# Rotary embedding on one core: all DMAs through one ring, and the tables as 16 descriptors of 4 KB

## The chip, the cores and the metric

One core of a Trainium2 chip runs the kernel. The metric is the device time of one execution in microseconds (us). Besides that there is one profiled execution, whose span (first to last instruction) and own time are given below.

## What is computed

The input `x` is 16 x 512 x 1024 float32 (batch, position, 16 heads of 64). Each head's 64 values are two halves of 32, which are rotated by tables `cos` and `sin` of 512 positions x 32:

```python
x = x.reshape(batch, seq, num_heads, head_dim)
x1, x2 = x[..., :half_dim], x[..., half_dim:]
cos = cos[None, :, None, :]
sin = sin[None, :, None, :]
rotated = np.concatenate([
    x1 * cos - x2 * sin,
    x1 * sin + x2 * cos
], axis=-1)
```

Input and output are 33.55 MB each; each table is 64 KB.

## The kernel before

**Slabs.** The work is cut into eight slabs of 4 MB, numbered 0 to 7. A slab is 128 partitions x 8192 float32: 8 rows of 1024 in each partition. Three places on chip (`places`, L52) hold a pair of neighbouring slabs each: 0 and 1, 2 and 3, 4 and 5. Slabs 6 and 7 use the first place again, so loads 6 and 7 have to wait until stores 0 and 1 have left it. In DRAM a partition's 16 rows of a pair lie together (`there`, L59), so a DMA of one slab has 32 KB in each partition, and a DMA of a pair 64 KB.

**A slab's way.** ScalarE casts the slab from float32 to bf16 in place (`cast`, L132, by `copy`, L137). VectorE makes two multiplications with the tables (L152) and one addition of swapped halves (L155). ScalarE casts the result back to float32, into the same place (L158), and the slab is stored. Slab 0 is worked on in two parts of 4 rows, slab 7 in parts of 4, 2 and 2. ScalarE's casts are in an order written out by hand: the cast of the next slab stands ahead of the back-cast of the present one, so each of its rounds is cast(s+1), back-cast(s); for slab 7 all casts come ahead of the back-cast of slab 6.

**Tables.** `cos` and `sin` are loaded with 64 partitions x 1 KB each (L77 to L79), which is 8 positions in a partition. GpSimd builds selection matrices (`pick`, L87 to L95) and casts each table to bf16 (L99). TensorE spreads them to 128 partitions: for each parity of slab four matmuls with `pick` as weights (L106), into the column layout cos, cos, sin, -sin; -1 in `pick` makes the sign. VectorE copies the even slabs' table to bf16 (L113), ScalarE the odd slabs' (L144). No multiplication can start before the first copy.

**Queues and their order.** SyncE (SP) and ScalarE (ACT) each feed a ring of their own, and 16 DMA engines take packets from both. On SP: load 0, load 1, loads 2 and 3 in two DMAs of every second partition (L83), loads 4 and 5 in one DMA, all issued without a wait, then load 6 behind store 0, and load 7 behind store 1. On ACT: the tables (L78) at the start, then the stores of slabs 0 to 3 (L69), each behind its slab's back-cast in ScalarE's own sequence, the pair 4 and 5 in two halves (L162) and the pair 6 and 7 in one DMA.

The part of the changed function that sets the queues is short:

```python
def load(s, n=1):
    nc.sync.dma_start(out=here(s, n), in_=there(x, s, n))

def store(s, n=1):
    nc.scalar.dma_start(out=there(out_flat, s, n), in_=here(s, n))
```

Of the kernel before, what the change touches and what calls it, by code (L numbers as in the profile page):

```python
# [2 lines left out]

# [4 lines left out]


@with_exitstack  # L10
def kernel(
    ctx: ExitStack,
    tc: tile.TileContext,
    x: bass.AP,
    cos: bass.AP,
    sin: bass.AP,
    num_heads: int,
    out: bass.AP,
):
    nc = tc.nc  # L20
    P = nc.NUM_PARTITIONS

    batch, seq, dim = x.shape
    nh = num_heads
    hd = dim // nh
    half = hd // 2
    bf16 = mybir.dt.bfloat16
    f32 = mybir.dt.float32

    nb = 2  # L30
    nslabs = batch // nb
    rpp = nb * seq // P
    W = rpp * dim
    TP = seq // rpp
    TW = rpp * half

    out_flat = out.rearrange("b s h d -> b s (h d)")

    singles = ctx.enter_context(tc.tile_pool(name="singles", bufs=1))
    pairs = ctx.enter_context(tc.tile_pool(name="pairs", bufs=3))  # L40
    psum = ctx.enter_context(tc.tile_pool(
        name="psum", bufs=1, space=bass.MemoryType.PSUM))


    def view(t, offset, *dims):
        return dataclasses.replace(t, offset=t.offset + offset,
                                   ap=[t.ap[0], *[list(d) for d in dims]])

    places = [pairs.tile([P, 2 * W], f32, tag="pair", name="pair") for _ in range(3)]  # L52


    def here(s, n=1):
        return view(places[s // 2 % 3], s % 2 * W, (1, n * W))


    def there(t, s, n=1):  # L59
        return bass.AP(tensor=t.tensor, offset=t.offset + s // 2 * 2 * P * W + s % 2 * W,  # L60
                       ap=[[2 * W, P], [1, n * W]])


    def load(s, n=1):
        nc.sync.dma_start(out=here(s, n), in_=there(x, s, n))  # L65


    def store(s, n=1):
        nc.scalar.dma_start(out=there(out_flat, s, n), in_=here(s, n))  # L69


    load(0)


    cos_sb = singles.tile([TP, TW], f32, tag="cos_sb")
    sin_sb = singles.tile([TP, TW], f32, tag="sin_sb")
    for t, src in ((cos_sb, cos), (sin_sb, sin)):  # L77
        nc.scalar.dma_start(out=t, in_=bass.AP(  # L78
            tensor=src.tensor, offset=src.offset, ap=[[TW, TP], [1, TW]]))  # L79

    load(1)
    for p in range(2):
        nc.sync.dma_start(out=here(2, 2)[p::2], in_=there(x, 2, 2)[p::2])  # L83
    load(4, 2)


    pick = singles.tile([TP, 4 * P], bf16, tag="pick")  # L87
    nc.gpsimd.memset(pick, 0.0)  # L88
    for h in range(2):
        for g in range(2):  # L90
            part = view(pick, (2 * h + g) * P, (TP // 2, 2 * P // TP), (1, TP // 2))
            nc.gpsimd.affine_select(  # L92
                out=part, in_=part, compare_op=mybir.AluOpType.not_equal,
                fill=1.0 - 2.0 * g, base=-h, pattern=[[0, 2 * P // TP], [-2, TP // 2]],
                channel_multiplier=1)  # L95

    tab1 = singles.tile([TP, 2 * TW], bf16, tag="tab1")
    for i, t in enumerate((cos_sb, sin_sb)):
        nc.gpsimd.tensor_copy(out=view(tab1, i * TW, (1, TW)), in_=t)  # L99

    accs, tabs = [], []
    for h in range(2):
        acc = psum.tile([P, 2 * rpp * hd], f32, tag=f"acc{h}", name="acc")
        for i in range(2):
            for f in range(2):
                nc.tensor.matmul(  # L106
                    view(acc, i * rpp * hd + f * half, (hd, rpp), (1, half)),
                    view(pick, (2 * h + i * f) * P, (1, P)),
                    view(tab1, i * TW, (half, rpp), (1, half)),
                    start=True, stop=True)  # L110
        accs.append(acc)
        tabs.append(singles.tile([P, 2 * rpp * hd], bf16, tag=f"tab{h}", name="tab"))
    nc.vector.tensor_copy(out=tabs[0], in_=accs[0])  # L113

    passes = []
    for s in range(nslabs):
        r = 0  # L120
        for n in {0: (4, 4), nslabs - 1: (4, 2, 2)}.get(s, (rpp,)):
            passes.append((s, r, n))
            r += n


    def halves(u):
        s, r, n = u
        t = here(s).bitcast(bf16)
        return [view(t, (2 * r + i * n) * dim, (1, n * dim)) for i in range(2)]


    def cast(u):  # L132
        s, r, n = u
        copy(halves(u)[0], view(here(s), r * dim, (1, n * dim)))


    def copy(out, in_):  # L137
        tc.keep_in_program_order(nc.scalar.copy(out=out, in_=in_))  # L138


    ahead = list(passes)
    for _ in range(2):
        cast(ahead.pop(0))
    copy(tabs[1], accs[1])  # L144
    cast(ahead.pop(0))
    for i, u in enumerate(passes):
        s, r, n = u
        while ahead and len(passes) - len(ahead) < (i + 2 if s < nslabs - 2 else len(passes)):
            cast(ahead.pop(0))
        lo, up = halves(u)  # L150
        for t, a in ((up, 0), (lo, rpp * hd)):
            nc.vector.tensor_mul(  # L152
                out=t, in0=lo,
                in1=view(tabs[s % 2], a + r * hd, (hd, n), (0, nh), (1, hd)))
        nc.vector.tensor_add(  # L155
            out=up, in0=up, in1=view(lo, half, (hd, n * nh), (-half, 2), (1, half)))

        copy(view(here(s), r * dim, (1, n * dim)), up)  # L158
        if r + n == rpp:
            if s == 5:  # L160
                for p in range(2):
                    nc.scalar.dma_start(out=there(out_flat, 4, 2)[p::2], in_=here(4, 2)[p::2])  # L162
            elif s == 7:
                store(6, 2)
            elif s < 4:
                store(s)
            if s < 2:
                load(s + 6)


# [1 line left out]
_INS = ['x', 'cos', 'sin', 'num_heads']  # L172
_OUTS = [((16, 512, 16, 64), 'float32')]

_NUMBERS = {'num_heads': 16}


# [26 lines left out]
```

## Time and profile before

| what | value |
|---|---|
| median of 3 runs | 161.87 us (161.72 to 161.93) |
| profiled execution, its own time | 161.8 us |
| its span | 160.0 us |
| VectorE busy | 107.9 us (67%) |
| ScalarE busy | 114.3 us (71%) |
| packets of SP's queue (q1), share of 16 engines | 49.5% |
| packets of ACT's queue (q10), share of 16 engines | 48.7% |
| bytes moved | 67.24 MB, mean 420 GB/s |
| one cast of a slab on ScalarE | 7.02 us |
| one multiplication or addition of a slab on VectorE | 4.42 us |

The page's part 3 gives, for each DMA queue, the time of its packets as a share of 16 engines over the span. The trace has a record of each packet: queue, size, start and duration. A packet of 32 KB took 1.213 us (median), one of 64 KB 2.418, one of 1 KB 0.046. The windows view counts the packets that start in a stretch; its last two columns are the busy share of the 16 DMA engines and GB/s. Before them it gives, for each engine, the busy time in the stretch and the number of instructions, and the granted TensorE clock, 1.00 throughout. When a DMA has landed, the engine that waits for it starts some 0.9 us later (load 0's completion packets from 12.30 us, its cast at 13.35).

### The profile page before, as it was taken

What the parts mean: (1) busy time and instruction counts of PE and PEld (TensorE: products, weight loads), DVE (VectorE), ACT (ScalarE), POOL (GpSimd) and SP (SyncE); (2) the same over time, 40 slices, a digit from 0 to 9 for tenths busy, and PEclk for the clock granted to TensorE, in tenths of its full rate; (3) what the DMA queues carried; (4) which work ended last, traced back from release to release, by engine and by line L of the source; (5) the groups of instructions that cost most, each with busy time, mean ns of one, the idle gap of its engine ahead of it and who ended that gap; (6) DMA issues with size and microseconds to landing.
All of it is one profiled execution on the core that took longest, in us unless ns stands there. A gap on an engine that the chain in (4) does not pass through costs nothing.

```text
span 160.0 us, 167 instructions
## 1 busy us (share of the span) xinstructions
PE 2.0 (1%) x8; PEld 1.0 (1%) x8; DVE 107.9 (67%) x34; ACT 114.3 (71%) x24; POOL 2.6 (2%) x11
## 2 busy tenths in 40 slices
PE   0001300000000000000000000000000000000000
PEld 0000100000000000000000000000000000000000
DVE  0000499999951999799889979998999998000000
ACT  3006959993089989998998999999879999500000
POOL 4000000000000000000000000000000000000000
DMA  7999999699599999999999999999997999989966
GB/s 262 401 401 410 426 491 524 262 524 524 254 401 410 606 426 393 393 393 393 467 451 393 434 483 393 401 500 410 393 590 328 524 393 393 524 360 426 524 262 262
DMA packets 1920, 67.24 MB, mean 420 GB/s; under 512 B 256, under 2 KB 384, under 8 KB 384
## 3 DMA queue, kind: packets, MB, share of 16 engines
q1 hardware_dynamic: 880, 33.55, 49.5%
q10 hardware_dynamic: 1040, 33.69, 48.7%
HBM read 33.69 MB, written 33.55 MB: 420 GB/s over the span
## 4 chain that ended last, share of the span: by engine, by line
ACT 52%; DMA 26%; issue 5%; ACTq 1%; SPq 1%; another core or an unknown queue 0%
ACT pair L138 52%; DMA pair<-in_x_dram 26%; ACTq L162 1%; ACTq L69 1%; SPq L65 0%; SPq L83 0%; ACTq L138 0%
## 5 line engine op out<-in xcount | busy, mean ns | idle before, releaser
L138 ACT CAST pair<-pair 128x8192 bf16<-128x8192 f32 (+5 forms) x22 | 112.1, 5155 | 21.9 <-DMA pair<-in_x_dram 19.8
L152 DVE TENSOR_TENSOR pair<-pair,tab 128x8192 bf16<-128x8192 bf16 (+2 forms) x22 | 71.4, 3259 | 9.3 <-ACT pair L138 8.9
L155 DVE TENSOR_TENSOR pair<-pair 128x8192 bf16<-128x8192 bf16 (+2 forms) x11 | 35.8, 3260 | 0.3
L113 DVE CAST tab<-acc 128x1024 bf16<-128x1024 f32 x1 | 1.2, 1225 | 18.3 <-PE acc L106 18.3
L138 ACT ACT_TABLE_LOAD x1 | 1.3, 1283 | 2.0 <-issue 2.0
L106 PE MATMUL acc<-tab,pick 64*128 64x256 bf16 x8 | 2.0, 403 | 17.1 <-POOL tab L99 17.1
L106 PEld LDWEIGHTS <-pick 64*128 64x128 bf16 x8 | 1.0, 127 | 17.6 <-issue 15.6
L92 POOL TENSOR_SCALAR_AFFINE_SELECT pick<-pick 64x128 bf16<-64x128 bf16 x4 | 1.1, 303 | 0.1
L138 ACT CAST tab<-acc 128x1024 bf16<-128x1024 f32 x1 | 1.0, 1004 | 0.0
L99 POOL CAST tab<-cos_sb 64x256 bf16<-64x256 f32 x1 | 0.4, 391 | 9.5 <-DMA cos_sb<-in_cos_dram 9.5
L88 POOL MEMSET pick<- 64x512 bf16 x1 | 0.5, 519 | 0.3 <-POOLq L185 0.3
L99 POOL CAST tab<-sin_sb 64x256 bf16<-64x256 f32 x1 | 0.4, 396 | 4.9 <-DMA sin_sb<-in_sin_dram 4.9
L185 POOL MEMSET const-float32-0.0<- 128x1 f32 x1 | 0.1, 104 | 0.2 <-issue 0.2
L185 POOL MEMSET const-bfloat16-1.0<- 128x1 bf16 x1 | 0.1, 107 | 0.0
L185 POOL MEMSET const-uint8-127<- 128x1 uint8 x1 | 0.1, 107 | 0.0
L185 POOL MEMSET const-float32-1.0<- 128x1 f32 x1 | 0.1, 104 | 0.0
## 6 DMA issues: line engine op xcount, KB each, us to landing
pair<-in_x_dram SPq DMA_DIRECT2D x4, 4096.0 KB, 22.5
out_dram<-pair ACTq DMA_DIRECT2D x4, 4096.0 KB, 32.8
cos_sb<-in_cos_dram ACTq DMA_DIRECT2D x1, 64.0 KB, 11.1
sin_sb<-in_sin_dram ACTq DMA_DIRECT2D x1, 64.0 KB, 15.8
pair<-in_x_dram SPq DMA_DIRECT2D x3, 42.2
out_dram<-pair ACTq DMA_DIRECT2D x3, 21.0
```

The source lines that it names most:

```text
L69: nc.scalar.dma_start(out=there(out_flat, s, n), in_=here(s, n))
L88: nc.gpsimd.memset(pick, 0.0)
L92: nc.gpsimd.affine_select(out=part, in_=part, compare_op=mybir.AluOpType.not_equal, fill=1.0 - 2.0 * g, base=-h, pattern=[[0, 2 * P // TP] ...
L99: nc.gpsimd.tensor_copy(out=view(tab1, i * TW, (1, TW)), in_=t)
L106: nc.tensor.matmul(view(acc, i * rpp * hd + f * half, (hd, rpp), (1, half)), view(pick, (2 * h + i * f) * P, (1, P)), view(tab1, i * TW, ( ...
L113: nc.vector.tensor_copy(out=tabs[0], in_=accs[0])
L138: tc.keep_in_program_order(nc.scalar.copy(out=out, in_=in_))
L152: nc.vector.tensor_mul(out=t, in0=lo, in1=view(tabs[s % 2], a + r * hd, (hd, n), (0, nh), (1, hd)))
L155: nc.vector.tensor_add(out=up, in0=up, in1=view(lo, half, (hd, n * nh), (-half, 2), (1, half)))
L162: nc.scalar.dma_start(out=there(out_flat, 4, 2)[p::2], in_=here(4, 2)[p::2])
L185: nc = _bacc.Bacc("TRN2", target_bir_lowering=False, num_devices=1)
```

## The change

All DMAs go through SP's ring, in this order: load 0, the tables, load 1, loads 2 and 3 (two halves), store 0, loads 4 and 5, store 1, load 6, store 2, load 7, store 3, stores 4 and 5 (two halves), stores 6 and 7. They are held in program order. SP thus waits for each store's back-cast, and for the places of loads 6 and 7, with the later DMAs behind it. Loads 4 and 5, which waited for nothing, now stand behind store 0.

Each table is loaded as 16 partitions x 4 KB, 32 positions in a partition: `cos` to partitions 0, 8, ... 120 and `sin` to 4, 12, ... 124 of one tile `raw`, which VectorE clears first, so that the partitions between hold zeros; the table DMAs wait for that. GpSimd casts `raw` (128 x 1024) as a whole. The matmuls take all 128 partitions, with six selection matrices in place of four, and each target is now the sum of two matmuls (`m` = 0, 1), since a slab's rows lie in two column ranges: 16 matmuls in place of 8, eight per table. In the built program VectorE's first six operations on slab 0 are four multiplications and then two additions; before, they were three multiplications, an addition, a multiplication and an addition.

```diff
     def load(s, n=1):
-        nc.sync.dma_start(out=here(s, n), in_=there(x, s, n))
+        tc.keep_in_program_order(nc.sync.dma_start(out=here(s, n), in_=there(x, s, n)))

     def store(s, n=1):
-        nc.scalar.dma_start(out=there(out_flat, s, n), in_=here(s, n))
+        tc.keep_in_program_order(
+            nc.sync.dma_start(out=there(out_flat, s, n), in_=here(s, n)))

+    TR = 16
+    TC = seq * half // TR
+    raw = singles.tile([P, TC], f32, tag="raw")
+    nc.vector.memset(raw, 0.0)
     load(0)
-    cos_sb = singles.tile([TP, TW], f32, tag="cos_sb")
-    sin_sb = singles.tile([TP, TW], f32, tag="sin_sb")
-    for t, src in ((cos_sb, cos), (sin_sb, sin)):
-        nc.scalar.dma_start(out=t, in_=bass.AP(
-            tensor=src.tensor, offset=src.offset, ap=[[TW, TP], [1, TW]]))
+    for i, src in enumerate((cos, sin)):
+        to = dataclasses.replace(
+            raw, offset=raw.offset + 4 * i * raw.ap[0][0],
+            ap=[[P // TR * raw.ap[0][0], TR], [1, TC]])
+        tc.keep_in_program_order(nc.sync.dma_start(out=to, in_=bass.AP(
+            tensor=src.tensor, offset=src.offset, ap=[[TC, TR], [1, TC]])))

     load(1)
     for p in range(2):
-        nc.sync.dma_start(out=here(2, 2)[p::2], in_=there(x, 2, 2)[p::2])
-    load(4, 2)
+        tc.keep_in_program_order(
+            nc.sync.dma_start(out=here(2, 2)[p::2], in_=there(x, 2, 2)[p::2]))

-    pick = singles.tile([TP, 4 * P], bf16, tag="pick")
+    pick = singles.tile([P, 6 * P], bf16, tag="pick")
     nc.gpsimd.memset(pick, 0.0)
-    for h in range(2):
-        for g in range(2):
-            part = view(pick, (2 * h + g) * P, (TP // 2, 2 * P // TP), (1, TP // 2))
+    for g in range(3):
+        for m in range(2):
+            part = view(pick, (g * 2 + m) * P + m, (2 * TR, P // TR // 2), (2, TR))
             nc.gpsimd.affine_select(
                 out=part, in_=part, compare_op=mybir.AluOpType.not_equal,
-                fill=1.0 - 2.0 * g, base=-h, pattern=[[0, 2 * P // TP], [-2, TP // 2]],
-                channel_multiplier=1)
+                fill=-1.0 if g == 2 else 1.0, base=-4 if g else 0,
+                pattern=[[0, P // TR // 2], [-(P // TR), TR]], channel_multiplier=1)

-    tab1 = singles.tile([TP, 2 * TW], bf16, tag="tab1")
-    for i, t in enumerate((cos_sb, sin_sb)):
-        nc.gpsimd.tensor_copy(out=view(tab1, i * TW, (1, TW)), in_=t)
+    raw_b = singles.tile([P, TC], bf16, tag="raw_b")
+    nc.gpsimd.tensor_copy(out=raw_b, in_=raw)
...
-        for i in range(2):
-            for f in range(2):
+        for g, at in ((0, 0), (0, half), (1, rpp * hd), (2, rpp * hd + half)):
+            for m in range(2):
                 nc.tensor.matmul(
-                    view(acc, i * rpp * hd + f * half, (hd, rpp), (1, half)),
-                    view(pick, (2 * h + i * f) * P, (1, P)),
-                    view(tab1, i * TW, (half, rpp), (1, half)),
-                    start=True, stop=True)
+                    view(acc, at, (hd, rpp), (1, half)),
+                    view(pick, (g * 2 + m) * P, (1, P)),
+                    view(raw_b, (2 * m + h) * TW, (half, rpp), (1, half)),
+                    start=m == 0, stop=m == 1)
...
             if s == 5:
                 for p in range(2):
-                    nc.scalar.dma_start(out=there(out_flat, 4, 2)[p::2], in_=here(4, 2)[p::2])
+                    tc.keep_in_program_order(nc.sync.dma_start(
+                        out=there(out_flat, 4, 2)[p::2], in_=here(4, 2)[p::2]))
...
-            if s < 2:
-                load(s + 6)
+            if s < 3:
+                load(*((4, 2), (6,), (7,))[s])
```

More of the change, by code (lines that the diff above doesn't have):

```diff
@@ L33 @@
     W = rpp * dim
-    TP = seq // rpp
     TW = rpp * half
```

## The prediction

> **What bounds the kernel now.** I read the page's first three parts, then the windows view cut at the stages of the DMA traffic, then the timelines of ScalarE and SyncE. The page:
>
> ```profile
> span 160.0 us, 167 instructions
> ...
> PE 2.0 (1%) x8; PEld 1.0 (1%) x8; DVE 107.9 (67%) x34; ACT 114.3 (71%) x24; POOL 2.6 (2%) x11
> ...
> DMA  7999999699599999999999999999997999989966
> ...
> q1 hardware_dynamic: 880, 33.55, 49.5%
> q10 hardware_dynamic: 1040, 33.69, 48.7%
> HBM read 33.69 MB, written 33.55 MB: 420 GB/s over the span
> ```
>
> No engine is busy for more than 71%, but the packets of the two DMA queues together fill 98.2% of 16 engines' span. The dips in the DMA row are an artefact: a packet is counted in the slice in which it starts, and 16 engines start 64 KB packets nearly together. The chain of waits names ScalarE for 52% and a load for 26%; that chain is carried by the DMA engines, since ScalarE's waits end when loads land. The windows view, with edges where a batch of packets starts (last two columns: busy share of the DMA engines, GB/s):
>
> ```profile
> 1.70:3.50 1.80, 0.00 (x0) 0.08 (x1) 0.00 (x0) 1.28 (x1) 0.71 (x3) 1.00 1.04 291
> 3.50:16.30 12.80, 0.58 (x2) 0.25 (x2) 0.00 (x0) 2.95 (x1) 0.39 (x1) 1.00 1.00 420
> 16.30:22.35 6.05, 1.43 (x6) 0.67 (x5) 3.96 (x3) 5.07 (x3) 0.40 (x1) 1.00 1.01 433
> 22.35:39.29 16.94, 0.00 (x0) 0.00 (x0) 16.87 (x7) 14.04 (x3) 0.00 (x0) 1.00 1.00 433
> 39.29:42.27 2.98, 0.00 (x0) 0.00 (x0) 2.94 (x2) 0.00 (x0) 0.00 (x0) 1.00 1.02 352
> 42.27:71.20 28.93, 0.00 (x0) 0.00 (x0) 22.66 (x6) 26.30 (x4) 0.00 (x0) 1.00 1.00 435
> 71.20:119.68 48.48, 0.00 (x0) 0.00 (x0) 45.51 (x11) 46.16 (x8) 0.00 (x0) 1.00 1.00 433
> 119.68:158.40 38.72, 0.00 (x0) 0.00 (x0) 15.92 (x10) 18.49 (x7) 0.00 (x0) 1.00 1.00 433
> ```
>
> The reader is to see one rate: 433 GB/s with loads alone (22.35 to 39.29), 433 with stores alone (from 119.68), 433 to 435 with both queues taking turns (42.27 to 119.68). Loads and stores together are 67.11 MB, so 67.11 MB / 433 GB/s = 155.0 us is spent whatever the order. The packets run from 1.73 to 158.85 us, 157.1 us. The 2.1 us above 155.0 lie in three places. (a) The first load packets: 0.52 MB in 1.80 us instead of 1.21, **0.6 us**. (b) The stretch with the tables: ten batches of loads, 5.24 MB, need 12.11 us and took 12.80, **0.69 us**. (c) The batch ahead of the first store: 1.05 MB in 2.98 instead of 2.42 us, **0.56 us**. Completion packets (9 ns each, one per engine and DMA) make up the rest. Nothing is gained outside these three.
>
> **The change part by part.**
>
> *Tables.* Before: 128 packets of 1 KB, eight per engine, 46 ns each in the packet records: 0.37 us of the 0.69. The other 0.32 is load packets beside them that took 1.27 to 1.33 us instead of 1.21. After: two packets of 4 KB per engine. The records give 1.213 us for 32 KB and 2.418 for 64 KB, so 36.8 ns per KB and 8 ns each, and 4 KB comes to 0.155 us. Two, and two completions, make 0.33. Ends of the unknown disturbance: nothing (saving 0.36) or all of the old price again (saving 0). There is one junction in place of eight, so I take the disturbance of one, 0.06, and a **saving of 0.30 us**.
>
> [...] The rows: the old tables went to partitions 0 to 63 and took 46 ns per KB, on the same line as the large packets to all 128. [...]
>
> *All stores on SP's ring.* Bytes and packet sizes stay. Rates are equal for one queue and two, so the move itself is worth 0. What can change is (c), and whether the ring ever runs dry. In order the ring ends its entries at: load 0 12.1, tables 12.5, load 1 22.2, loads 2 and 3 41.5, store 0 51.8 with (c) kept, loads 4 and 5 71.1, store 1 80.8, load 6 90.5, store 2 100.2, load 7 109.9, store 3 119.6, stores 4 and 5 139.0, stores 6 and 7 158.4. (8 packets per slab and engine at 1.21 us; 9.7 us a slab.)
>
> *Is each entry issued in time?* An issue takes 1.0 us to its first packet (0.74 to 1.73 for load 0). ScalarE's casts are 7.02 us a slab, and start 0.9 us behind a landing. Load 1 lands at 22.2: cast 1 from 23.1 to 30.1, the two back-casts of slab 0 to 37.3. Store 0 is due at 41.5: 3.2 us of cover. SP holds loads 4 and 5 behind it, due at 51.8, so they are late only if store 0 is. Cast 2 starts at 42.4 (44.49 before), so store 1 is issued at 56.5, due 71.1. Load 6 then waits for store 0's landing (about 53), which is over. Store 2 follows at 70.5, due 90.5. Load 7 waits for store 1's landing at about 82; store 3 queues behind that wait, but isn't ready before 86; both are due from 100.2 on. Loads 4 and 5 land at 71.1: cast 4 at 72.0 (73.41 before), then six casts to 114.1: stores 4 and 5, due 119.6. The last store: before, it was issued at 138.21 and its first packet followed at 139.1, without a gap.
>
> ```profile
> 115.58 1.22 ACTq L162 DMA_DIRECT2D out_dram<-pair  x2
> 116.83 21.34 ACT L138 CAST pair<-pair 128x4096 bf16<-128x4096 f32 x7 [1.29 <-issue]
> 138.21 0.34 ACTq L69 DMA_DIRECT2D out_dram<-pair  x1
> ```
>
> ScalarE starts that chain 1.4 us earlier and no longer issues stores inside it (0.34 + 1.22 us), though VectorE's last adds hold it by up to 0.6. I expect the issue near 136.2, due 139.0: 1.8 us of cover after the 1.0 to the first packet. Gone, each further us costs one.
>
> *The table path.* VectorE's clearing of 128x1024 is not in the trace; the nearest row, a cast of that shape on it, took 1.23 us. Thus cos is issued near 2.0, sin 2.5, load 1 3.1, all behind load 0, which runs to 12.1. The tables land at 12.5, GpSimd starts at 13.4. Its cast of 1024 columns: four times the 0.39 us of 256 is 1.56, the least is one fixed cost less, 1.2; I take 1.4. Eight matmuls by 0.24 us (six took 1.43): 2.0. VectorE's copy 1.23: first multiplication near 18.1, against 19.58. Its order now has four multiplications ahead of the first sum, five by 2.28 us, so the first sum is ready at 29.5 and the back-cast can't start before 30.1. Hidden; it would have to be 3.8 us late to delay store 0 past its cover. Longer pick building on GpSimd (six selections by 0.3, a larger memset, at most 3 us in all) lies ahead of 13.4.
>
> **Sum.** The profiled execution took 161.8 us with a span of 160.0: 161.8 - 0.30 = **161.5 us**; the median shown is 161.87, 0.07 above that execution, which is within the spread of the runs (161.72 to 161.93).
>
> **Rivals.**
>
> *(c) goes too.* If 0.56 us is the price of a second queue that starts in full traffic, one ring doesn't pay it: 161.5 - 0.6 = 160.9. For: no later change of direction pays. Against: it may be the first write to the output, which stays; packets of the second queue (the tables) began at 5.97 without a loss. Chance 0.30.
>
> *The tables cost as much as before.* Load packets beside them lose 0.3 us again, or the 4 KB packets, each into a single partition, run at half rate (2 x 0.155 = 0.31 us more): 161.8 to 161.9. For: 0.32 us of the old price was disturbance. Against: it came with eight interleaved packets. [...] Chance 0.12.
>
> *Slower: a toll at each change of direction within one ring.* [...] After, the ring changes seven times. If an engine can't prepare across a change, (c) is that toll, paid seven times instead of once: 6 x 0.56 = 3.4, or 164.9; if only load to store pays, 3 x 0.56 = 1.7, or 163.2. For: the one change seen without a primed second queue cost 0.56. Against: the turns by packet cost nothing for 77 us. It decides as soon as a change costs over 0.05 us. [...] Chance 0.15.
>
> *A late last store or late tables:* cover of 1.8 and 3.2 us gone, 0.5 us slower at 162.4. Chance 0.03.
>
> **How the numbers follow.** Forecast 0.40. This kernel's measurement can tell about 0.2% (0.32 us) from no change. The forecast sits at that edge: 0.23 faster, 0.17 same. With (c) gone 0.30 faster; tables as before 0.12 same; toll and lateness 0.18 slower. Faster 0.53, same 0.29, slower 0.18. Range: 160.9 less the runs' half spread, 160.7, to a store half a us late on tables at the old price, 162.4; the tolls are left out. The likeliest case alone: 161.4 to 161.8.
>
> **What would show it.** One queue with all bytes; a windows view at 433 GB/s from 22 us to the end; the last packets end near 158.5. A window of 2 to 3 us at 350 around 41.5 shows (c) kept, none shows it gone; dips at 51.8, 71, 81, 90, 100, 110 and 120 show the toll. VectorE's first multiplication near 18; last store issued near 136. The prediction is wrong if any stretch after 22 us falls below 430 beside these.

## The result and the profile after

The changed kernel takes 162.83 us (median of 6 runs, 162.47 to 163.53), the kernel before 161.84 (6 runs, 161.72 to 161.93): a ratio of 1.0064, 95% interval 1.0049 to 1.0079. It is 1.0 us slower where 0.3 us faster was forecast, and lies above the forecast's range of 160.7 to 162.4. Its runs scatter five times as much. The page of the profiled execution (162.84 us):

```profile
span 161.0 us, 195 instructions
...
PE 3.6 (2%) x16; PEld 2.3 (1%) x16; DVE 108.7 (67%) x35; ACT 114.0 (71%) x24; POOL 3.3 (2%) x12
...
DMA  7999999969499996999999999999997997997991
...
q1 hardware_dynamic: 1824, 67.24, 98.0%
HBM read 33.69 MB, written 33.55 MB: 418 GB/s over the span
```

One queue now has all the bytes, and its packets fill 98.0% of the 16 engines' span: the DMA engines are still the bound. They don't idle either: by the packet records no engine has a gap of more than 0.06 us between two load or store packets from 22 us to the end. So the time must have gone into packets that took longer. The windows view, cut at the first engine's start of each batch:

```profile
3.30:22.00 18.70, 3.57 (x16) 2.16 (x15) 5.44 (x3) 8.02 (x3) 1.04 (x1) 0.99 1.00 428
...
22.00:38.95 16.95, 0.00 (x0) 0.00 (x0) 16.92 (x7) 14.04 (x3) 0.00 (x0) 0.50 1.00 433
38.95:42.78 3.83, 0.00 (x0) 0.00 (x0) 3.80 (x2) 0.00 (x0) 0.00 (x0) 0.50 1.00 274
42.78:52.46 9.68, 0.00 (x0) 0.00 (x0) 3.34 (x2) 8.74 (x2) 0.00 (x0) 0.50 1.00 433
52.46:71.78 19.32, 0.00 (x0) 0.00 (x0) 18.72 (x5) 19.04 (x3) 0.00 (x0) 0.50 1.00 434
```

The reader is to see 433 GB/s before and behind one batch, and 274 in it. That batch is the last load packets of slabs 2 and 3, ahead of store 0: 1.05 MB in 3.83 us instead of 2.42, a dip of 1.4 us where the kernel before had 0.56. The engines and SyncE's issues are not late. The timeline of SyncE:

```profile
37.01 0.35 SPq L70 DMA_DIRECT2D out_dram<-pair  x1
37.41 0.43 SPq L65 DMA_DIRECT2D pair<-in_x_dram  x1
57.69 0.34 SPq L70 DMA_DIRECT2D out_dram<-pair  x1
58.13 0.38 SPq L65 DMA_DIRECT2D pair<-in_x_dram  x1
71.53 0.34 SPq L70 DMA_DIRECT2D out_dram<-pair  x1
82.82 0.33 SPq L65 DMA_DIRECT2D pair<-in_x_dram  x1
86.73 0.34 SPq L70 DMA_DIRECT2D out_dram<-pair  x1
114.42 1.63 SPq L167 DMA_DIRECT2D out_dram<-pair  x2
137.04 0.35 SPq L70 DMA_DIRECT2D out_dram<-pair  x1
```

Each DMA is issued before the ring gets to it: store 0 at 37.0 for 41.4, the last one at 137.0 for 139.5. VectorE's first multiplication starts at 17.79.

A second loss hardly shows in a rate. The records of the packets give the time by which each took longer than its usual 1.213 or 2.418 us. Summed and divided by 16, it is 1.39 us in the batch ahead of the first store, and 0.17 in all that follows, nearly all of it in the last load packets ahead of store 1 (69.5 us), store 2 (90) and store 3 (109.6). At these three places some engines lose up to 0.33 us and others nothing. Nothing brings them together again. The engines' starts in one batch spread over 0.40 us ahead of store 0 and 0.50 behind it. One load packet at 55.3 us, which took 0.11 us longer on the latest engine, makes that 0.56; it is 0.57 behind store 1, 0.88 behind store 2 and 1.04 behind store 3, constant in between. The last packets end from 158.84 to 159.88 us, against 158.45 to 158.85 before. The slowest engine sets the end: 1.03 us later, of which 0.66 is the mean of the engines and 0.37 their spread.

### The profile page after: what moved, and what is told of

It is laid out like the page before. It is cut to its first block, busy times and chain, and to the rows that moved or that the text cites. A ratio compares the mean times of both kernels' runs of the same rounds, so it can differ in the third digit from the quotient of the medians.

```text
span 161.0 us, 195 instructions
## 1 busy us (share of the span) xinstructions
PE 3.6 (2%) x16; PEld 2.3 (1%) x16; DVE 108.7 (67%) x35; ACT 114.0 (71%) x24; POOL 3.3 (2%) x12
## 4 chain that ended last, share of the span: by engine, by line
DMA 34%; ACT 29%; DVE 12%; issue 8%; ACTq 1%; SPq 1%
DMA pair<-in_x_dram 34%; ACT pair L143 29%; DVE pair L157 10%; ACTq L205 1%; DVE pair L160 1%; SPq L83 1%; DVE raw L77 1%; SPq L70 0%; ACTq L143 0%
## 5 line engine op out<-in xcount | busy, mean ns | idle before, releaser
L157 DVE TENSOR_TENSOR pair<-pair,tab 128x8192 bf16<-128x8192 bf16 (+2 forms) x22 | 71.3, 3259 | 10.0 <-ACT pair L143 9.7
L111 PE MATMUL acc<-raw_b,pick 128*128 128x256 bf16 x16 | 3.6, 414 | 14.6 <-POOL raw_b L104 14.6
L111 PEld LDWEIGHTS <-pick 128*128 128x128 bf16 x16 | 2.3, 142 | 15.4 <-issue 12.6
L77 DVE MEMSET raw<- 128x1024 f32 x1 | 0.9, 912 | 1.0 <-PEq L191 1.0
L98 POOL TENSOR_SCALAR_AFFINE_SELECT pick<-pick 128x64 bf16<-128x64 bf16 x6 | 1.3, 263 | 0.1
L104 POOL CAST raw_b<-raw 128x1024 bf16<-128x1024 f32 x1 | 1.0, 1037 | 10.6 <-DMA raw<-in_sin_dram 10.6
L94 POOL MEMSET pick<- 128x768 bf16 x1 | 0.7, 738 | 0.3 <-POOLq L191 0.3
```

Of the source, the lines that this page charges most:

```text
L77: nc.vector.memset(raw, 0.0)
L98: nc.gpsimd.affine_select(out=part, in_=part, compare_op=mybir.AluOpType.not_equal, fill=-1.0 if g == 2 else 1.0, base=-4 if g else 0, pat ...
L104: nc.gpsimd.tensor_copy(out=raw_b, in_=raw)
L111: nc.tensor.matmul(view(acc, at, (hd, rpp), (1, half)), view(pick, (g * 2 + m) * P, (1, P)), view(raw_b, (2 * m + h) * TW, (half, rpp), (1 ...
L157: nc.vector.tensor_mul(out=t, in0=lo, in1=view(tabs[s % 2], a + r * hd, (hd, n), (0, nh), (1, hd)))
```

## The experiments

The tables below use two numbers from the packet records. A **dip** is the excess of load and store packets over their usual time, mean over the 16 engines, "first" in the batch ahead of store 0, "later" in all that follows. (By this count the dip before is 0.61, by the window 0.56.) **Ends** are the first and the last engine's last packet. Dips, ends and span are those of one profiled execution. Each ratio is to the kernel before as it ran beside that kernel, where its median was 161.69 to 161.93 us.

| kernel | rings | median us, ratio to before (interval) | first dip | later dips | ends | span |
|---|---|---|---|---|---|---|
| before | 2 | 161.84 | 0.61 | 0.01 | 158.45 to 158.85 | 160.0 |
| before, 2nd profile | 2 | 161.54, one run | 0.06 | 0.04 | 158.24 to 158.58 | 159.8 |
| before, 3rd profile | 2 | 162.21, one run | 0.77 | 0.07 | 158.84 to 159.25 | 160.4 |
| tables alone | 2 | 162.12, 0.9993 (0.9959 to 1.0026) | 1.02 | 0.05 | 158.76 to 159.20 | 160.4 |
| old tables in SP's ring | 2 | 161.80, 0.9998 (0.9987 to 1.0009) | 0.48 | 0.01 | 158.41 to 158.85 | 160.0 |
| new tables in ACT's ring | 2 | 161.89, 1.0012 (0.9996 to 1.0028) | 0.04 | 0.39 | 158.34 to 159.22 | 160.4 |
| changed | 1 | 162.83, 1.0064 (1.0049 to 1.0079) | 1.39 | 0.17 | 158.84 to 159.88 | 161.0 |
| changed, 2nd profile | 1 | 163.25, one run | 0.91 | 0.30 | 158.72 to 160.26 | 161.4 |
| changed, 3rd profile | 1 | 163.73, one run | 0.87 | 0.69 | 158.79 to 160.73 | 161.9 |
| ring alone | 1 | 163.15, 1.0106 (1.0029 to 1.0182) | 0.35 | 0.41 | 158.36 to 159.83 | 161.0 |
| early write | 1 | 163.77, 1.0116 (1.0063 to 1.0169) | 1.28 | 0.26 | 158.99 to 161.61 | 162.9 |
| early write, same region | 1 | 163.57, 1.0118 (1.0098 to 1.0138) | 0.72 | 0.63 | 158.91 to 160.38 | 161.6 |
| whole load | 1 | 163.50, 1.0113 (1.0093 to 1.0133) | 1.20 | 0.81 | 159.09 to 160.74 | 162.0 |
| loads 4, 5 first | 1 | 162.31, 1.0027 (1.0014 to 1.0041) | 0.37 | 0.19 | 158.20 to 159.08 | 160.2 |
| two changes | 1 | 162.34, 1.0035 (1.0021 to 1.0049) | 0.90 | 0.10 | 158.49 to 159.51 | 160.7 |

**Tables alone.** The tables of the changed kernel, in SP's ring behind load 0; the other DMAs in the queues of the one before. The diff is against the changed kernel.

```diff
     def store(s, n=1):
-        tc.keep_in_program_order(
-            nc.sync.dma_start(out=there(out_flat, s, n), in_=here(s, n)))
+        nc.scalar.dma_start(out=there(out_flat, s, n), in_=here(s, n))
...
+    load(4, 2)
...
-            if s < 3:
-                load(*((4, 2), (6,), (7,))[s])
+            if s < 2:
+                load(s + 6)
```

> The tables' part alone: 16 descriptors of 4 KB per table behind load 0 in SP's ring, clearing, selection and matmuls as in the changed kernel; the stores stay in ACT's ring and loads 4 and 5 are issued without a wait, as before. All theories of the lost microsecond put it at the first store in SP's ring, so this kernel should keep the old dip of about 0.56 us around the first store and save 0.2 to 0.4 us on the tables: 161.5 us, ratio to before 0.998. If the tables' new form (clearing, longer matmuls, lower granted TensorE clock) is what costs, it is 162.5 or more.

162.12 us against 161.87, and the interval can't tell it from no change. The expected gain isn't there, and the first dip was 1.02, not 0.56. Yet this is 0.7 us below the changed kernel, and no dip follows. The tables' form isn't what costs the 1.0 us.

**Ring alone.** The tables as before, in ACT's ring, all else in SP's in the changed order. The diff is against the kernel before.

```diff
     def store(s, n=1):
-        nc.scalar.dma_start(out=there(out_flat, s, n), in_=here(s, n))
+        tc.keep_in_program_order(
+            nc.sync.dma_start(out=there(out_flat, s, n), in_=here(s, n)))
...
-    load(4, 2)
...
-            if s < 2:
-                load(s + 6)
+            if s < 3:
+                load(*((4, 2), (6,), (7,))[s])
```

> The ring alone: loads and stores in SP's ring in the changed kernel's order, the tables as before (64 partitions of 1 KB, in ACT's ring). Both theories: the dip at the first store is 1.4 us as in the changed kernel, and the tables keep their old price of 0.7, so 163.1 us, ratio 1.008. If the changed tables are needed for the loss, 161.9.

163.15 us, as expected, so one ring in this order is what costs. But the reason given was wrong: the first dip was 0.35, not 1.4. The time lies in later dips (0.41) and in ends that spread over 1.47 us.

**Early write.** A first theory was that the first write to the output is slow. This kernel and the next four are the changed kernel with one more edit, shown against it where nothing else is said.

```diff
     load(1)
+    zero = singles.tile([P, P], f32, tag="zero")
+    nc.vector.memset(zero, 0.0)
+    tc.keep_in_program_order(nc.sync.dma_start(
+        out=bass.AP(tensor=out_flat.tensor, offset=out_flat.offset + 6 * P * W,
+                    ap=[[2 * W, P], [1, P]]), in_=zero))
```

> The changed kernel with one small write more: 512 bytes from each of 128 partitions to slab 6's region of the output, in SP's ring behind load 1 (later overwritten by the last store); it adds about 0.3 us of packets. Theory 1, the first write to the output is slow wherever it comes: a dip of 0.6 to 1.4 us appears around 22 us and the one at 39 to 43 is gone; time 162.8 to 163.2. Theory 2, a store that is issued while only few packets are left in its ring stalls it: no dip at 22, since that write is queued 18 us ahead, and 1.4 us still at 39 to 43; time about 163.1. The stretches tell, not the time.

The windows view of this kernel, first the batch with the small write, then the one ahead of store 0:

```profile
20.81:22.23 1.42, 0.00 (x0) 0.00 (x0) 1.42 (x1) 0.26 (x1) 0.00 (x0) 0.50 0.90 380
39.13:42.70 3.57, 0.00 (x0) 0.00 (x0) 3.54 (x2) 0.00 (x0) 0.00 (x0) 0.50 1.04 294
```

1.42 us is a batch of loads (1.21) and the 0.2 of the small write's own packets; the dip stays at 39 us. The theory of a first write falls, unless the region matters. That was the next one.

**Loads 4 and 5 first.** The rival: a store that is issued shortly before its turn stalls the ring.

```diff
+    load(4, 2)
...
-            if s < 3:
-                load(*((4, 2), (6,), (7,))[s])
+            if s in (1, 2):
+                load(s + 5)
```

> The changed kernel with loads 4 and 5 ahead of store 0 in SP's order, so that store 0 is issued near 37 us but due at about 61 us, some 23 us ahead. Theory 1, the first write is slow: the dip of 1.4 us moves to about 61 us, and the time stays at 162.8. Theory 2, a store that comes late into a ring with few packets left: no dip anywhere after 22 us, time 161.3 to 161.5.

```profile
39.25:58.59 19.34, 0.00 (x0) 0.00 (x0) 14.32 (x4) 15.80 (x3) 0.00 (x0) 0.50 1.00 434
58.59:61.40 2.81, 0.00 (x0) 0.00 (x0) 2.78 (x2) 2.81 (x1) 0.00 (x0) 0.50 0.99 373
```

The stretch in which the dip had stood runs at 434 now, and the dip has moved with the store to 58.6 us. It isn't gone, though store 0 was issued at 37.5, 21 us ahead: lateness isn't the cause either. It is smaller (0.37), and with three changes from load to store in place of four the kernel is 0.5 us faster than the changed one; which of the two made it faster, this kernel doesn't tell.

**Same region, whole load, two changes.** Three more variants. The small write went to slab 0's own region (the diff is against the early write):

```diff
-        out=bass.AP(tensor=out_flat.tensor, offset=out_flat.offset + 6 * P * W,
+        out=bass.AP(tensor=out_flat.tensor, offset=out_flat.offset,
```

> The changed kernel with a small early write as in the run before, but into slab 0's own region of the output (512 bytes at the start of each of its 128 rows, later overwritten by store 0). Theory A, the first touch of the region that is stored to is slow: the dip of 1.3 to 1.4 us at 39 to 43 us shrinks below 0.3 us and appears around 22 us instead. Theory B, a change from loads to stores within one ring delays each engine's last load packet by an amount that differs by engine and is largest at the first real store: the dip stays at 0.4 to 1.4 us. Time 163 to 163.6 by B.

Loads 2 and 3 went in one DMA of 128 partitions:

```diff
-    for p in range(2):
-        tc.keep_in_program_order(
-            nc.sync.dma_start(out=here(2, 2)[p::2], in_=there(x, 2, 2)[p::2]))
+    load(2, 2)
```

> The changed kernel with loads 2 and 3 in one DMA of 128 partitions in place of two of every second partition. Theory C, the half-partition loads ahead of the first store make it stall: the dip shrinks to the 0.02 to 0.14 us of the later changes, time near 161.6. Theory B: the dip stays at 0.4 to 1.4 us, time 162.5 to 163.

And all loads but 6 and 7 went ahead of store 0, those two behind store 1:

```diff
+    load(4, 2)
...
-            if s < 3:
-                load(*((4, 2), (6,), (7,))[s])
+            if s == 1:
+                load(6)
+                load(7)
```

> The changed kernel with loads 4 and 5 ahead of store 0, and loads 6 and 7 together behind store 1: two changes from load to store in place of four, and store 0 issued some 20 us before it is due. Theory B: first change 0.4 us as in the kernel with loads 4 and 5 first, one later change of 0.1, engines' ends within 0.5 us: 161.5 to 162.0 us, below the 162.3 of that kernel with three changes. If the changes don't matter, 162.3 as there.

The batch ahead of the first store in each of the three, same region first:

```profile
39.35:42.53 3.18, 0.00 (x0) 0.00 (x0) 3.15 (x2) 0.00 (x0) 0.00 (x0) 0.50 0.99 330
```

```profile
39.14:42.66 3.52, 0.00 (x0) 0.00 (x0) 3.49 (x2) 0.00 (x0) 0.00 (x0) 1.00 1.03 298
```

```profile
58.49:61.75 3.26, 0.00 (x0) 0.00 (x0) 3.23 (x2) 3.26 (x1) 0.00 (x0) 1.00 1.02 322
```

The dip is in all three, 0.72, 1.20 and 0.90. The region and the half-partition loads are cleared. Two changes gave 162.34, like three (162.31), not the 161.5 to 162.0 expected: its first dip was 0.90 and not 0.4. Its one later change cost 0.09, and there the engines' spread grew from 0.7 to 1.0 us.

**More changes.** Stores 0 to 2 and the loads behind them were cut into halves of every second partition that alternate, seven changes in place of four; in a second kernel VectorE's operations were held in program order as well.

```diff
-                store(s)
-            if s < 3:
-                load(*((4, 2), (6,), (7,))[s])
+                if s < 3:
+                    to = ((4, 2), (6, 1), (7, 1))[s]
+                    for p in range(2):
+                        tc.keep_in_program_order(nc.sync.dma_start(
+                            out=there(out_flat, s)[p::2], in_=here(s)[p::2]))
+                        tc.keep_in_program_order(nc.sync.dma_start(
+                            out=here(*to)[p::2], in_=there(x, *to)[p::2]))
+                else:
+                    store(s)
```

> The changed kernel with stores 0 to 2 and the loads behind each of them cut into two halves that alternate in the ring (every second partition each, packets of the same size): seven changes from load to store in place of four. Theory B: each added change costs another 0.02 to 0.15 us on average over the engines and spreads their ends further, so 163.2 to 163.8 us. If only the first store matters, 162.8 as the changed kernel.

> The kernel with seven changes from load to store in place of four again, now with VectorE's operations held in program order (in the earlier run they had changed their order and VectorE waited). Theory B: three changes more at 0.1 to 0.4 us each on the slowest engine: 163.2 to 164.3 us, the engines' starts spread by 1.5 us or more at the end. If the number of changes doesn't matter: 162.5 to 163.0 with a spread of 1.0 as in the changed kernel.

217.24 and 216.43 us: both miss their question. In the first, VectorE took slab 2 ahead of slab 1 and stood idle for 18.8 us; in the second it waited for a half store of slab 0, the only slab whose store had been issued by then, to land before it could start on slab 1, the next in its order. The timeline:

```profile
63.23 8.89 DVE L157 TENSOR_TENSOR pair<-pair,tab 128x8192 bf16<-128x8192 bf16 x2 [31.51 <-DMA out_dram<-pair]
```

So this program waits for a DMA of every second partition of a slab as if it touched the neighbouring slab too. What more changes cost in time was not measured. One added change came while the ring was still full, from the first half of loads 4 and 5 to the second half of store 0: its last load packets, at 54 to 55 us, lost 0.11 us on the mean engine in the first kernel and 0.09 in the second.

**Old tables in SP's ring, new tables in ACT's ring.** Why was the first dip larger with the tables alone than before? One theory was a store ring that nothing has used yet. The first diff is against the kernel before, the second against the tables alone.

```diff
-        nc.scalar.dma_start(out=t, in_=bass.AP(
+        nc.sync.dma_start(out=t, in_=bass.AP(
             tensor=src.tensor, offset=src.offset, ap=[[TW, TP], [1, TW]]))
```

> The kernel before with only its two table loads (old form, 64 partitions of 1 KB) moved from ACT's ring to SP's, behind load 0; stores stay in ACT's ring. If a store ring that nothing has used yet makes the first store dearer (theory D), the dip at the first store is 1.0 us as with the tables alone, not 0.6, and the time is 161.9 to 162.2. If not, the dip stays near 0.6 and the time is 161.4 to 161.7, since the tables no longer disturb the packets of load 0.

```diff
-        tc.keep_in_program_order(nc.sync.dma_start(out=to, in_=bass.AP(
-            tensor=src.tensor, offset=src.offset, ap=[[TC, TR], [1, TC]])))
+        nc.scalar.dma_start(out=to, in_=bass.AP(
+            tensor=src.tensor, offset=src.offset, ap=[[TC, TR], [1, TC]]))
```

> The kernel with the tables alone, but the 16 descriptors of 4 KB go through ACT's ring, as the old tables did. Theory D, the unused ring: the dip at the first store is back near 0.6 us, time 161.5 to 161.7. If the new form of the tables or the earlier start of VectorE goes with the larger dip, it stays at 1.0 us, time 162.0 to 162.2.

An unused ring had a dip of 0.48 where the kernel before, with a used one, had 0.61: the theory of the unused ring falls by that. The other used ring had 0.04, and the size starts to look like chance. Neither kernel differs from before by more than its interval. The second has the only later dips of a two-ring kernel (0.39, from 73 to 91 us). Of these, 0.32 lie in load packets around 88.4 to 89.9 us, where no engine has a store packet: store 1 is over and store 2 hasn't begun. So this loss, too, is one of loads just ahead of a store. Why it came here is not explained, since in the other two-ring profiles no such place cost more than 0.01.

**Held load.** Is a change inside one ring needed? Two rings, but made to take turns in time:

```diff
-    load(4, 2)
...
+        if i == 2:
+            copy(view(places[2], 0, (1, 1)), view(here(2), 0, (1, 1)))
+            load(4, 2)
...
-            if s < 2:
-                load(s + 6)
+            if s == 1:
+                load(6)
+                load(7)
```

> The kernel before, two rings, but loads 4 and 5 are held back until ScalarE has cast slab 2 (a one-column copy into their place, which they overwrite), so that store 0 runs alone in ACT's ring, then loads alone in SP's, and store 1 starts into loads alone again near 60 us. Theory B1, an engine can't prepare across a change inside one ring: no loss at 60 us, since two rings are in use. Theory B2, writes that start while all engines only read delay those reads, whichever ring they come from: a dip of 0.3 to 1.4 us summed over the batch near 60 us, as at the first store. The time itself is 163 to 172 us, since the ring runs empty for a while and the loads come later.

168.36 us, as the ring runs empty for a while. What counts is its windows view: the batch ahead of store 0, then one of loads alone, the next, which is the last ahead of store 1, and the mix behind it.

```profile
39.57:42.03 2.46, 0.00 (x0) 0.00 (x0) 2.46 (x1) 0.00 (x0) 0.00 (x0) 1.00 1.01 426
57.96:60.39 2.43, 0.00 (x0) 0.00 (x0) 2.40 (x2) 2.02 (x2) 0.00 (x0) 1.00 1.00 432
60.39:63.61 3.22, 0.00 (x0) 0.00 (x0) 3.22 (x1) 3.22 (x1) 0.00 (x0) 1.00 0.98 326
63.61:81.73 18.12, 0.00 (x0) 0.00 (x0) 14.34 (x4) 10.72 (x3) 0.00 (x0) 1.00 1.00 434
```

In this kernel the first store came almost free (0.06), and the second, which starts into loads alone again, cost 0.74, between 0.63 and 0.93 on each engine. So a change inside one ring is not needed, and the first store isn't special: a store that starts while all engines only load can delay their current load packets, whichever ring it comes from. Once loads and stores take turns packet by packet, the mix in this kernel shows no loss (434 GB/s).

**Both kernels again.** Two more profiles of each, for the size of the dip.

> The changed kernel once more, for a second profile. If the size of the dip at the first store belongs to the kernel's form, it is 1.4 us again (mean over the engines), and the later changes from load to store cost 0.02 to 0.1 each. If it varies from run to run, it lies anywhere from 0.05 to 1.4, and the time follows the sum of the dips and the spread of the engines' ends: 162.3 to 163.5 us.

> The changed kernel, a third profile: as the second. In both cases the engines' ends should be spread by 0.9 us or more, since that has held for nearly every one-ring kernel so far.

> The kernel before once more, for a second profile. By its form: a dip of 0.6 us at the first store again. If it varies from run to run: 0.05 to 0.8. In both cases no further dip behind it and the engines' ends spread by 0.4 to 0.5 us, since the two rings mix loads and stores from then on; 161.6 to 162.1 us.

> The kernel before, a third profile: the dip at the first store is 0.6 us again, or anywhere from 0.05 to 0.8; none behind it; ends spread by 0.4 to 0.5 us.

The windows view of the third profile of the changed kernel, at the four changes and one clean stretch:

```profile
39.26:42.42 3.16, 0.00 (x0) 0.00 (x0) 3.13 (x2) 0.00 (x0) 0.00 (x0) 1.00 1.04 332
...
69.00:71.65 2.65, 0.00 (x0) 0.00 (x0) 2.65 (x1) 2.34 (x1) 0.00 (x0) 1.00 1.05 396
71.65:89.80 18.15, 0.00 (x0) 0.00 (x0) 15.72 (x5) 16.72 (x3) 0.00 (x0) 1.00 1.00 433
89.80:91.04 1.24, 0.00 (x0) 0.00 (x0) 1.24 (x1) 1.24 (x1) 0.00 (x0) 1.00 1.14 423
...
109.20:110.58 1.38, 0.00 (x0) 0.00 (x0) 1.38 (x1) 1.38 (x1) 0.00 (x0) 1.00 0.94 380
```

And of the second profile of the kernel before, ahead of the first store and behind it:

```profile
39.52:42.04 2.52, 0.00 (x0) 0.00 (x0) 2.52 (x1) 0.00 (x0) 0.00 (x0) 1.00 0.98 416
42.04:118.23 76.19, 0.00 (x0) 0.00 (x0) 67.41 (x17) 71.08 (x11) 0.00 (x0) 1.00 1.00 434
```

The size varies from run to run: 0.06, 0.61 and 0.77 in the same kernel before, 0.87, 0.91 and 1.39 in the same changed kernel. What doesn't vary is what follows. With two rings in the kernel before, 76 us at 434 GB/s and ends within 0.41 us; with one ring, three more dips and ends over 1.04 to 1.94 us. The granted TensorE clock has no part in it: from 22 us on it was 0.50 in the first profile of the changed kernel and 1.00 in the third, and the dips are in both.

The packet records show one thing more in those 76 us: the rings don't mix throughout. Between one store and the next each engine runs two load packets in a row. So for 4.3, 1.9 and 1.9 us (67.0 to 71.3, 88.7 to 90.6 and 106.9 to 108.8 in the first profile) no engine has a store packet, and then stores start into loads alone. In the six profiles of the kernel before, the tables alone, the old tables in SP's ring and the new ones in ACT's there are 18 such places: 17 cost at most 0.01 us, and one the 0.32 told above. In the changed kernel loads are alone for 9 to 19 us ahead of stores 1 to 3, and these changes cost 0.02 to 0.38 us.

By the means of three profiles each, the last end moves by 1.40 us, from 158.89 to 160.29. Of this, the first dip gives 0.58 (0.48 to 1.06), the later ones 0.35 (0.04 to 0.39), the tables' stretch gives back 0.20 and the rest 0.06. That is 0.67 on the mean engine; the slowest engine's distance from the mean, 0.28 before and 1.00 after, gives the other 0.7. The two single runs of the changed kernel were slower than its median by 0.4 and 0.9 us, so the sum is somewhat more than the 1.0 us of the comparison.

## Why the prediction was wrong

**What bounds.** Right. The DMA engines are full in both kernels, and 433 to 434 GB/s holds with one queue, with two, with loads alone and with stores alone.

**Tables, saving 0.30.** Right in kind, too large. The 4 KB packets took 0.159 us, just what 8 ns and 36.8 ns per 1,000 bytes give for 4,096 bytes; the 0.155 worked out took them as 4,000. The term that was too small is the disturbance of the load packets beside them: 0.06 was put down, and they lost 0.15 to 0.30 in the three profiles. With the disturbance of the load packets the price of the stretch was 0.78 us on average over three profiles before and 0.58 over three after: 0.20 saved. No run shows the half rate for packets into a single partition that the rival "The tables cost as much as before" put at 0.31 us more: all 32 of them took 0.159 (at most 0.222 in the two later profiles). What all 16 engines on one table at once would give isn't shown: they reach the tables over 0.4 us, and at most some ten were on one table at a time. A fifth of a us is less than the first dip varies by itself, so no kernel here shows the gain in its time.

**Issue times.** Right. VectorE's first multiplication 17.79 (18.1 worked out), store 0 issued at 37.0 (37.3), the last at 137.0 (136.2); store 1 at 57.7 (56.5) because the dip delayed the landing of slabs 2 and 3. No entry came late, and the ring never ran dry.

**(c), "with (c) kept" at 0.56.** Wrong. One profile gave 0.56 and I took it for a price of the kernel. It is a draw from 0.06 to 0.77 with this kernel's two rings, and was 0.87 to 1.39 in three draws with one. In all one-ring kernels it lies between 0.35 and 1.39, in two-ring kernels between 0.04 and 1.02: larger on average, but the ranges overlap. The rival "(c) goes too" missed as well: one ring didn't remove the dip.

**"Rates are equal for one queue and two, so the move itself is worth 0."** This step failed. The rates are equal within a direction, and in mixed traffic. What the move adds is three more changes of all engines from a long stretch of loads alone to stores. The kernel before doesn't have them: from 42 us on its two rings mix both, but for the three stretches of 1.9 to 4.3 us. Counted over three profiles each, the later dips are 0.35 us more on the mean engine, and the slowest engine's distance from the mean, which the sum had no term for, is 0.7 more. I had read those 77 us without a loss as evidence that a change is free; they show that mixed traffic, and a change behind a few us of loads, cost nothing in that kernel.

**The toll rival, 0.15.** It had the right sign and, in its half "only load to store pays", the right places. Its price was wrong: 0.56 at each change, 163.2. That this lies within 0.4 us of the measured 162.83 is luck. Measured, a later change cost 0.02 to 0.38 us on the mean engine in the changed kernel's three profiles. The rest came by a way that the rival didn't have: a change hits the engines unequally, and the slowest sets the end. Its reason, that an engine can't prepare across a change within one ring, isn't needed, as the held load shows (0.74 us with two rings), and it doesn't fit the changes from stores to loads inside the one ring, which had no loss: packets start 1.21 us apart across the first of them (51.26 to 52.47 in the changed kernel). Ahead of the first change from loads to stores, the last load packets of loads 2 and 3 took up to 1.59 us longer in the same profile.

**What stays open.** What in the chip delays a load packet when stores start, why the size varies for the same kernel (the first dip of the kernel before from 0.06 to 0.77 us), and why the engines lose unequal amounts at the later changes. That a change is free behind 1.9 to 4.3 us of loads alone and costs behind 9 or more is only read off the kernels at hand; the length was not varied by itself, and of the three later changes the one behind 19 us was not the dearest in each profile. The order of the changes was not permuted, so whether the first is larger because it is first, or because stores come into the longest run of loads, wasn't tried.

## What to carry to other kernels

Where the DMA engines are the bound, as here (their packets fill 98.0% of the span), look at how often stores start into a long run of loads. In the kernel before, two queues of opposite direction mixed loads and stores packet by packet (434 GB/s over 76 us), so that it happened only once; in the changed kernel a single ring in the order of the work had it at each of stores 0 to 3, and each such change delayed some engines (0.02 to 0.38 us on the mean engine at the later three), which didn't catch up: the last packets ended over 1.04 to 1.94 us, against 0.34 to 0.41 before. Look at the spread of the engines' last packets, not only at the mean rate: in the first profile the rate was 433 to 434 GB/s over each of the stretches with the later losses. A term of half a us that one profile shows once is worth a second profile before a forecast is built on it.

## What was not expected of the hardware

- The engines drift: in the changed kernel the spread of their starts in one batch went 0.40, 0.50, 0.56, 0.57, 0.88, 1.04 us, with steps at the changes, one (0.56) amid loads, and level in between. In the kernel with the early write the slowest engine ended 2.2 us behind the mean (161.61 against 159.39).
- A change from stores to loads was free in the changed kernel's three profiles, where the load had been queued long before. In the held-load kernel the first load packets behind store 0 (52.5 us) lost 0.70 us; the load had been issued 1.0 us ahead and the engines had stood idle for 0.25 to 1.2 us. The idle time may be the reason: the very first load packets lose time as well, 0.66 us on the mean engine in the kernel before and 0.57 in the changed one.
- Descriptors of 4 KB, each to its own partition, took 0.159 us each, on the line of the large packets; 1 KB took 0.046.
